# A decoder layer on one core: where the weight sums of four Strassen-type units are made, and which queue loads them

## The chip, the cores and the metric

The kernel runs on one core of one Trainium2 chip. A core has a matrix engine (TensorE; PE in the profile, with its weight loads as PEld), three engines for elementwise work (VectorE = DVE, ScalarE = ACT, GpSimd = POOL), an engine that only issues transfers (SyncE = SP), and 16 DMA engines that all queues share. Every engine works its instructions in the order in which they were compiled, and an instruction that waits holds up all that stand behind it on its engine. The metric is device microseconds of one execution, the median of the runs.

## What is computed

One layer of a hybrid decoder on 512 tokens with 1024 channels, all in fp32:

```python
h = layer_norm(x, ln_in_g, ln_in_b)
q_g, k_g, v_g, r_g, a_lr, q_lat, kv_lat, gate_logits = jnp.split(h @ w_in, offsets, axis=-1)
...
y_gla = (rms_norm(gla_chunked(q_g, k_g, v_g, log_a)) * jax.nn.silu(r_g)) @ w_o_gla
y_mla = merge_heads(o_mla) @ w_o_mla
g_gla, g_mla = jnp.split(jax.nn.sigmoid(gate_logits + b_gate), N_BRANCH, axis=-1)
mix = (g_gla * y_gla + g_mla * y_mla) @ w_out
h = layer_norm(DEEPNORM_ALPHA * h + mix, ln1_g[l], ln1_b[l])
ff = jnp.square(jax.nn.relu(h @ w_ff1[l])) @ w_ff2[l]
h = layer_norm(DEEPNORM_ALPHA * h + ff, ln2_g[l], ln2_b[l])
```

Four column blocks of `h @ w_in`, each 1024 wide, matter here: `r_g` (the kernel's unit "r"), `v_g` ("v") and the two halves of `gate_logits` ("a" and "b").

## The kernel before

**Precision.** Each fp32 product is made of three products of rounded parts: every operand is split into a high part (rounded by ScalarE) and a low part (the rest, by VectorE). `pump` (L167) does this for weights: it issues the load into a raw tile `wraw` (L178, three buffers), then `whi` on ScalarE (L190) and `wlo` on VectorE (L191). A stream entry that has a `src` takes an existing tile instead of a load. Units r and v split up to two entries ahead and put some of the parts into tiles `xh`, `xl`; units a and b split one entry ahead into the two `whi` and two `wlo` buffers.

**The four units.** `unit(sec, nxt)` (L711) multiplies one block by a scheme that needs seven products in place of eight (Strassen's, in Winograd's form). The weight block is cut into four quarters, "11", "12", "21", "22", each 512 rows by 512 columns, and each quarter into two halves (`hf`) of 512 KB. The seven products n = 0 to 6 use the weight operands of

```python
RPH = ("T1", "11", "22", "T2", "21", "T3", "T4")
```

T1 is made of quarters 12 and 11, T2 of T1 and 22, T3 of 22 and 12, T4 of T2 and 21. "11" and "21" come through `pump` as `wraw`; the others live in tiles `rw`. A sum is made in place, by a transfer that GpSimd's queue issues and that adds what it reads to the tile (`accum_op=ALU.add`, L623); T1 and "22" begin with a plain load that SP issues (L625). So T1's tile becomes T2 and then T4, and the tile of "22" becomes T3. Each sum has to wait until the split of the tile's former content is done.

The token operands S1 to S4 are made once, by `r_sums` (L649), on VectorE and ScalarE, and `keep` stores copies of them in DRAM. Unit r reads the tiles that `r_sums` made; the other units get copies back by `fetch` (L644), two transfers of 512 KB each, into new tiles.

The units run in the order r, v, a, b. Within a unit the steps are written after the products: after n = 0 the sum T2 (with 22) and `fetch("S2")`; after n = 2 the sum T3; at n = 3 the next unit's T1 loads and sums (`r_begin`) and, after it, the sum T4; at n = 6 the next unit's "22" loads.

**What runs beside them.** Between the products of the units, `tick` advances generators: the levels of the four GLA heads (`gla_levels`, L872) and their outputs (`gla_out`, L970). At one level of each head the next head's decay sums are made: `totals` (L853) is a chain of ever shorter adds on GpSimd (`tot`, L859) with an exponential on ScalarE at its end (L863), and `products` (L865) puts two adds and multiplies on GpSimd (`pr` L867, `qkp` L870) with a ScalarE copy between them. The levels themselves are an ScalarE copy `M` (L902), a product on PE (`px`, L937), and VectorE steps (L884, L909).

**Order.** A planner in the framework orders each engine's instructions when the kernel is built, by a timeline of its own in which the instruction written earlier goes first among those that are ready, and gives tiles their places from pools. Most tiles of these stages (rw, S, xh, xl and others) share one pool of 24 places of 4 KB in each partition; an allocation waits until a place is free, which is when all uses of the former tile are done.

Of the kernel before, what the change touches and what calls it, by code (L numbers as in the profile page):

```python
# [16 lines left out]
ALU = mybir.AluOpType  # L17
# [3 lines left out]
T = 512  # L21
# [31 lines left out]
def tile_hybrid_block(ctx: ExitStack, tc: tile.TileContext, I, out, dbg=None):  # L53
    nc = tc.nc
# [18 lines left out]
    def A(shape, dt=F32, n="a"):  # L73
        tag, bufs = ("C", 8) if n in TAG_C else (n, TAG_W[n]) if n in TAG_W else ("A", 24)
        return pa.tile(shape, dt, tag=tag, bufs=bufs, name=nm(n))
# [17 lines left out]
    def f(ap):  # L93
        return ap.bitcast(F32)

    act = nc.scalar.activation
    vtt = nc.vector.tensor_tensor
# [46 lines left out]
    stream = []  # L144
# [22 lines left out]
    def pump(i):  # L167
        while st["dma"] < min(len(stream), i + 1 + DMA_AHEAD):
            e = stream[st["dma"]]
            st["dma"] += 1  # L170
            if "src" in e:
                continue
            raw = A([P, e["nk"], T * 2 // e["nk"]], F32, "wraw")
            for sl, src, cw in e["dmas"]:
                dst = raw[:, sl, :e["n"]]
                if cw is not None:
                    dst = dst.rearrange("p (h c) -> p h c", c=cw)
                nc.sync.dma_start(dst, src)  # L178
            e["raw"] = raw
        while st["spl"] < min(len(stream), i + 2 + SPLIT_AHEAD):  # L180
            e = stream[st["spl"]]
            if st["spl"] > i + e.get("ahead", SPLIT_AHEAD) and not e["res"]:
                break
            nk, n = e["nk"], e["n"]
            hi, lo = [A([P, nk, T * 2 // nk], F32R, w) for w in HOME["a" if e["res"] else e.get("home", "w")]]
            raw = e["src"]() if "src" in e else e.pop("raw")
            with ExitStack() as gates:
                for g in st["gates"]:
                    gates.enter_context(tc.issue_after(g.ins))
                st["ins"] = act(hi[:, :nk, :n], raw[:, :nk, :n], AF.Copy)  # L190
                vtt(lo[:, :nk, :n], raw[:, :nk, :n], f(hi[:, :nk, :n]), op=ALU.subtract)  # L191
            st["gates"] = ()
            e["w"] = (hi, lo)
            st["spl"] += 1

    def weights(pl, k):
        per = pl["per"]
        i = pl["idx"][k // per]
        pump(i)
        hi, lo = stream[i]["w"]  # L200
        return hi[:, k % per, :], lo[:, k % per, :]
# [16 lines left out]
    def tick(width):  # L218
        for g in list(active[:width or WID[0]]):
            step(g)  # L220
# [35 lines left out]
    def gemm_tm(pls, xs, n, evac, width=None, tts=range(NT), guard=None, ks=None, accs=None, new=None, fine=False):  # L256
# [29 lines left out]
        for i, (tt, j) in enumerate(todo):  # L286
            evac(tt, j, accs[tt, j])
            if i == len(todo) // 2 - 1:
                pump(pls[-1]["idx"][-1] + 1)
# [3 lines left out]
    PL = {}  # L293
# [10 lines left out]
    RW = {}  # L304
# [6 lines left out]
    for sec, i in ORDER:  # L311
        if sec in UNITS:
            c0 = UCOL[sec]
# [302 lines left out]
    def r_load(sec, op, i, j, hf, add=False):  # L616
        w = I["w_in"].rearrange("(k p) n -> p k n", p=P)
        if not add:
            RW[sec, op, hf] = A([P, 2, T], F32, "rw")
        k0 = 4 * i + 2 * hf  # L620
        c0 = UCOL[sec] + j * T
        if add:
            nc.gpsimd.dma_start(RW[sec, op, hf], w[:, k0:k0 + 2, c0:c0 + T], accum_op=ALU.add)  # L623
        else:
            nc.sync.dma_start(RW[sec, op, hf], w[:, k0:k0 + 2, c0:c0 + T])  # L625

    def r_begin(sec):
        for hf in range(2):
            r_load(sec, "T1", 0, 1, hf)
        r_add(sec, "T1", "T1", 0, 0)  # L630

    def r_add(sec, dst, src, i, j):
        for hf in range(2):
            RW[sec, dst, hf] = RW[sec, src, hf]
            r_load(sec, dst, i, j, hf, add=True)
# [8 lines left out]
    def fetch(name):  # L644
        RS[name] = [A([P, 4, 256], F32R, name) for _ in range(2)]
        for d, w in zip(KEPT[name], RS[name]):
            nc.sync.dma_start(f(w), f(d))
# [63 lines left out]
    def unit(sec, nxt=None):  # L711
        a, b = [[MM() for _ in range(2)] for _ in range(2)]
        R = {}
        val, gate, later = sec == "v", sec in "ab", sec != "r"
# [15 lines left out]
        def put(key, t, o, scale=1.0):  # L730
            act(home(key, t), view(o), AF.Copy, scale=scale)

        def last(key, t, o, op):
            r = home(key, t)
            vtt(r, r, view(o), op=op)
            if val:
                if t == 0:
                    R["v" + key] = [A([P, 2, T], F32R, n) for n in ("vh", "vl")]
                split(r, *[w[:, t] for w in R["v" + key]])
# [24 lines left out]
        def lhs(n, k, t):  # L764
            c = slice(0, 256) if t is None else slice(t * P, (t + 1) * P)
            d = slice(256 + c.start, 256 + c.stop)
            if n in (1, 4):
                h = hT[k + 4 * (n == 4)]
                return h[:, 0, c], h[:, 1, c]
            if n == 6:  # L770
                return hT[k + 4][:, 0, d], hT[k + 4][:, 1, d]
            key = {0: "S1", 2: "S4", 3: "S2", 5: "S3"}[n]
            while not later and key not in RS:
                step(t_rs)
            return [w[:, k, c] for w in RS[key]]

        for n in range(7):
            o = a if n in (1, 3, 5) else b
            for hf in range(2):
                pump(PL[sec, n, hf])  # L780
                opens = n in (0, 1, 4, 6) and hf == 0
                for pp in range(2):
                    opens = opens and pp == 0
                    closes = hf == 1 and pp == 1
                    hi, lo = [w[:, pp] for w in stream[PL[sec, n, hf]]["w"]]
                    if gate:
                        xh, xl = lhs(n, 2 * hf + pp, None)
                        for q in range(4):
                            c = slice(q * P, (q + 1) * P)
                            d = o[q // 2][:, q % 2 * 256:][:, :256]  # L790
                            mm(d, hi[:, c], xh, start=opens and q % 2 == 0, stop=False, skip_group_check=True)  # L791
                            mm(d, hi[:, c], xl, start=False, stop=False, skip_group_check=True)  # L792
                            mm(d, lo[:, c], xh, start=False, stop=closes, skip_group_check=True)  # L793
                        continue
                    for t in range(2):
                        xh, xl = lhs(n, 2 * hf + pp, t)
                        mm(o[t], xh, hi, start=opens, stop=False, skip_group_check=True)
                        mm(o[t], xh, lo, start=False, stop=False, skip_group_check=True)
                        mm(o[t], xl, hi, start=False, stop=closes, skip_group_check=True)
                if hf == 0 and (later or n in (0, 2, 4, 6)):  # L800
                    tick(None)
                if n == 0 and hf == 1:
                    r_add(sec, "T2", "T1", 1, 1)
                    if later:
                        fetch("S2")
                if n == 2 and hf == 1:
                    r_add(sec, "T3", "22", 0, 1)
                    if later:
                        fetch("S3")
                if n == 3 and hf == 1:  # L810
                    r_add(sec, "T4", "T2", 1, 0)
                if n == 3 and hf == 0 and nxt:
                    r_begin(nxt)
                if n == 5 and hf == 1 and nxt:
                    fetch("S1")
                if n == 0 and hf == 0 and later:
                    fetch("S4")
                if n == 6 and hf == 0 and nxt:
                    for h2 in range(2):
                        r_load(nxt, "22", 1, 1, h2)  # L820
            for t in range(2):
                if n == 0:
                    put("22", t, o[t], -1.0)
                elif n == 1:
                    put("11", t, o[t])
                elif n == 2:
                    put("12", t, o[t], -1.0)
                elif n == 3:
                    last("12", t, o[t], ALU.subtract)
                elif n == 4:  # L830
                    last("11", t, o[t], ALU.add)
                elif n == 5:
                    put("21", t, o[t])
                    last("22", t, o[t], ALU.subtract)
                else:
                    last("21", t, o[t], ALU.add)
            if n < 6:
                tick(None)
# [762 lines left out]
```

## Time and profile before

| what | value |
|---|---|
| median of 3 runs | 871.78 us (870.83 to 871.88) |
| the profiled execution | 871.12 us, its span 869.3 us |
| mean granted clock of TensorE | 0.995 |
| VectorE, ScalarE, GpSimd busy | 72%, 56%, 22% of the span |
| HBM read and written | 116.64 MB and 12.58 MB |

The profile is one execution recorded by the hardware. A row of the timeline gives the start and the length in us, the engine, the line, what is written and read (`rw<-in_w_in_dram`), and in brackets how long the engine sat idle before it and which event ended that wait. "x3" merges three instructions in a row; "SPq" is an instruction of SP's queue, where the length is the issue, not the transfer. A row of the windows gives a stretch of time, then its length, then each engine's busy time in it with the number of instructions, the granted clock of TensorE as a share of the full one, the mean busy share of the 16 DMA engines, and GB/s.

### The profile page before, as it was taken

How to read it: one execution, taken by the hardware profiler on the slowest of the kernel's cores; microseconds unless marked ns; L12 is line 12 of the kernel's file. 1: busy time of each engine (PE TensorE's matmuls, PEld its weight loads, DVE VectorE, ACT ScalarE, POOL GpSimd, SP SyncE). 2: the span in 40 equal slices, each digit the busy share in tenths (PEclk: the TensorE clock that was granted, in tenths of full speed). 3: DMA queues.
4: the chain of work that ended last, by engine and by line, in shares of the span. 5: the costliest groups of instructions: out<-in, count | busy, mean ns of one | idle time of the engine just before them, and what ended most of it. 6: DMA issues, size and time to landing. Idle time of an engine off the chain costs nothing. (4 is left out here: it accounts for less than half of the span.)

```text
span 869.3 us, 12408 instructions
## 1 busy us (share of the span) xinstructions
PE 850.9 (98%) x4594; PEld 736.0 (85%) x4594; DVE 630.1 (72%) x1023; ACT 485.7 (56%) x830; POOL 189.4 (22%) x220
## 2 busy tenths in 40 slices
PE   8999998999999999999999999999999999999995
PEld 5988777889999989888888888988888888888884
DVE  7967978988776657567766888986567546854687
ACT  5367757757674635455555324485366446745662
POOL 2304651625222210000000021005301520331023
PEclk9999999999999999999999999999999999999998
DMA  7746899998997614123136355008922990497075
GB/s 239 220 122 225 238 294 258 296 312 219 292 252 178 206 35 125 31 55 104 49 142 215 129 156 209 1 1 252 260 69 49 290 220 23 86 315 180 1 193 97
DMA packets 80924, 144.19 MB, mean 166 GB/s; under 512 B 9153, under 2 KB 35188, under 8 KB 80864
## 3 DMA queue, kind: packets, MB, share of 16 engines
q1 hardware_dynamic: 56480, 87.63, 29.8%
q0 software_dynamic: 22464, 52.11, 27.9%
q10 hardware_dynamic: 1920, 3.66, 1.3%
q8 instruction: 36, 0.59, 0.3%
q14 instruction: 24, 0.20, 0.1%
HBM read 116.64 MB, written 12.58 MB: 149 GB/s over the span
## 5 line engine op out<-in xcount | busy, mean ns | idle before, releaser
L191 DVE TENSOR_TENSOR wlo<-wraw,whi 128x1024 fp32r<-128x1024 f32 (+3 forms) x82 | 91.6, 1118 | 91.3 <-ACT whi L190 91.0
L190 ACT ACTIVATE whi<-wraw 128x1024 fp32r<-128x1024 f32 (+3 forms) x82 | 78.6, 959 | 62.7 <-PE mm L242 31.7
L242 PE MATMUL mm<-h,whi 128*128 128x512 f32 x288 | 112.1, 389 | 0.0
L241 PE MATMUL mm<-h,whi 128*128 128x512 f32 x288 | 112.1, 390 | 0.0
L243 PE MATMUL mm<-h,wlo 128*128 128x512 f32 x288 | 107.2, 389 | 0.0
L1463 POOL DMA_DIRECT2D res<-ev x54 | 47.7, 995 | 237.9 <-ACT ev L1461 194.3
L623 POOL DMA_DIRECT2D rw<-in_w_in_dram x32 | 39.7, 1240 | 110.4 <-DVE wlo L191 43.0
L243 PEld LDWEIGHTS mm<-h,wlo 128*128 128x128 f32 x288 | 54.0, 188 | 11.3
L241 PEld LDWEIGHTS mm<-h,whi 128*128 128x128 f32 x288 | 54.1, 188 | 11.1
L242 PEld LDWEIGHTS mm<-h,whi 128*128 128x128 f32 x288 | 54.1, 188 | 11.1
L191 DVE TENSOR_TENSOR wlo<-rw,whi 128x1024 fp32r<-128x1024 f32 x32 | 40.7, 1271 | 16.0 <-ACT whi L190 15.7
L1528 ACT ACTIVATE relu<-mm 128x512 f32<-128x512 f32 x32 | 18.8, 595 | 57.2 <-PE mm L243 57.2
L190 ACT ACTIVATE whi<-rw 128x1024 fp32r<-128x1024 f32 x32 | 33.8, 1057 | 18.7 <-PE mm L792 10.3
L382 POOL TENSOR_TENSOR mv<-mv,mhalf 128x1 f32<-128x1 f32 x4 | 4.1, 1035 | 169.3 <-DVE mv L381 169.3
L190 ACT ACTIVATE xh<-wraw 128x1024 fp32r<-128x1024 f32 (+1 forms) x24 | 23.3, 979 | 26.5 <-PE mm L276 15.2
L791 PE MATMUL mm<-S,whi 128*128 128x256 f32 x128 | 36.3, 288 | 0.0
L792 PE MATMUL mm<-S,whi 128*128 128x256 f32 x128 | 35.7, 283 | 0.0
L793 PE MATMUL mm<-S,wlo 128*128 128x256 f32 x128 | 34.5, 285 | 0.0
L191 DVE TENSOR_TENSOR wlo<-wq,whi 128x1024 fp32r<-128x1024 f32 x15 | 18.3, 1223 | 20.4 <-ACT whi L190 20.4
L191 DVE TENSOR_TENSOR xl<-wraw,xh 128x1024 fp32r<-128x1024 f32 (+1 forms) x24 | 26.2, 1110 | 5.9 <-ACT xh L190 5.9
L902 ACT ACTIVATE M<-qk 128x256 f32<-128x256 f32 x56 | 23.9, 456 | 8.4 <-DVE qk L884 7.5
L1461 ACT ACTIVATE ev<-mm 128x512 f32<-128x512 f32 x20 | 11.9, 601 | 27.8 <-DMA res<-ev 19.3
(473 smaller groups left out, 2730.4 us busy)
## 6 DMA issues: line engine op xcount, KB each, us to landing
rw<-in_w_in_dram POOLq DMA_DIRECT2D x32, 512.0 KB, 8.0
wraw<-in_w_ff_dram SPq DMA_DIRECT2D x32, 512.0 KB, 8.1
wq<-in_w_ff_dram POOLq DMA_DIRECT2D x32, 512.0 KB, 9.7
res<-ev POOLq DMA_DIRECT2D x54, 256.0 KB, 8.4
wraw<-in_w_in_dram SPq DMA_DIRECT2D x24, 512.0 KB, 5.0
S<-S SPq DMA_DIRECT2D x24, 512.0 KB, 6.7
rw<-in_w_in_dram SPq DMA_DIRECT2D x16, 512.0 KB, 8.7
S<-s SPq DMA_DIRECT2D x8, 512.0 KB, 5.1
```

What stands on the lines that cost most here:

```text
L190: st["ins"] = act(hi[:, :nk, :n], raw[:, :nk, :n], AF.Copy)
L191: vtt(lo[:, :nk, :n], raw[:, :nk, :n], f(hi[:, :nk, :n]), op=ALU.subtract)
L241: mm(o, hi[:, c], xh, start=first, stop=False)
L242: mm(o, hi[:, c], xl, start=False, stop=False)
L243: mm(o, lo[:, c], xh, start=False, stop=last)
L623: nc.gpsimd.dma_start(RW[sec, op, hf], w[:, k0:k0 + 2, c0:c0 + T], accum_op=ALU.add)
L791: mm(d, hi[:, c], xh, start=opens and q % 2 == 0, stop=False, skip_group_check=True)
L792: mm(d, hi[:, c], xl, start=False, stop=False, skip_group_check=True)
L793: mm(d, lo[:, c], xh, start=False, stop=closes, skip_group_check=True)
L902: act(packed(M, s, i), half_lr(qk, s, i), AF.Copy)
L1463: nc.gpsimd.dma_start(res[tt + t][:, j * T:(j + 1) * T], e, accum_op=ALU.add)
L1528: act(r, ps, AF.Relu)
```

## The change

```diff
@@ pump
             raw = e["src"]() if "src" in e else e.pop("raw")
+            e["was"] = raw
@@ r_load
         c0 = UCOL[sec] + j * T
+        by = nc.sync if sec in "ab" else nc.gpsimd
         if add:
             nc.gpsimd.dma_start(RW[sec, op, hf], w[:, k0:k0 + 2, c0:c0 + T], accum_op=ALU.add)
         else:
-            nc.sync.dma_start(RW[sec, op, hf], w[:, k0:k0 + 2, c0:c0 + T])
+            by.dma_start(RW[sec, op, hf], w[:, k0:k0 + 2, c0:c0 + T])
@@ unit
-                if n == 0 and hf == 1:
+                if n == 0 and hf == 1 and not gate:
                     r_add(sec, "T2", "T1", 1, 1)
+                if n == 1 and hf == 0 and gate:
+                    for h2 in range(2):
+                        t = RW[sec, "T2", h2] = RW[sec, "T1", h2]
+                        vtt(t, t, RW[sec, "22", h2], op=ALU.add)
                     if later:
                         fetch("S2")
...
-                if n == 3 and hf == 1:
+                if n == 3 and hf == 1 and not gate:
                     r_add(sec, "T4", "T2", 1, 0)
+                if n == 4 and gate:
+                    t = RW[sec, "T4", hf] = RW[sec, "T2", hf]
+                    vtt(t, t, stream[PL[sec, 4, hf]]["was"], op=ALU.add)
```

In the gate units a and b, T2 and T4 are now made by VectorE from tiles that lie in SBUF anyway: T2 = T1 + 22 from the two `rw` tiles, T4 = T2 + 21 from the `rw` tile and the raw tile `wraw` of quarter 21, which `pump` now remembers as `was`. That takes eight accumulating transfers of 512 KB away from GpSimd's queue (two sums, two halves, two units) and puts eight adds of 128x1024 elements on VectorE. T1 and T3 are still made by transfers.

In units r and v, the plain loads of T1 and "22" (two halves each, two units: eight transfers) are issued by GpSimd in place of SP. Units a and b keep theirs on SP.

`fetch("S2")` stands below the new condition now. In a and b it comes one entry later than before. In unit v it is gone: v reads the S2 tiles that `r_sums` made for unit r, which therefore keep two places of the pool until v's product n = 3 is done, and two transfers of 512 KB are not made.

## The prediction, made before the changed kernel ran

> **What bounds the kernel now.** I read the page's first part, then the windows of the four units, then the waits of PE alone, and last the timelines of the engines around the only long wait. The chain of waits is of no use here: it covers 2 us at the end.
>
> ```profile
> span 869.3 us, 12408 instructions
> PE 850.9 (98%) x4594; PEld 736.0 (85%) x4594; DVE 630.1 (72%) x1023; ACT 485.7 (56%) x830; POOL 189.4 (22%) x220
> ```
>
> PE is busy in 98% of the span. Nothing but a shorter PE wait can make this kernel faster; nothing but a new one can make it slower. The change removes no matmul. So the question is where PE waits inside the units. The lines of the first products say when r, v and a begin (first and last start); b begins at 243.4 by the timeline:
>
> ```profile
> L797 PE MATMUL mm<-whi,s x16: 387/389/467, 94.7 to 129.1; 128*128 128x512 f32 x16
> L797 PE MATMUL mm<-whi,S x16: 389/389/476, 145.0 to 177.3; 128*128 128x512 f32 x16
> L791 PE MATMUL mm<-S,whi x128: 274/283/365, 188.0 to 284.2; 128*128 128x256 f32 x128
> ```
>
> The windows cut there, of r, v, a and b in this order, tell how much waiting there is:
>
> ```profile
> 94.70:145.00 50.30, 47.14 (x228) 39.37 (x229) 41.34 (x67) 32.72 (x57) 22.75 (x30) 0.97 0.93 261
> 145.00:188.00 43.00, 43.00 (x213) 36.20 (x211) 40.74 (x56) 29.94 (x54) 16.93 (x19) 1.00 1.07 296
> 188.00:243.40 55.40, 55.13 (x461) 54.61 (x460) 44.95 (x66) 38.97 (x78) 20.04 (x20) 1.00 0.96 263
> 243.40:292.00 48.60, 48.60 (x411) 48.60 (x410) 33.16 (x49) 31.46 (x59) 11.58 (x13) 1.00 0.81 196
> ```
>
> The first figure behind the comma is PE's busy time. Unit r lacks 50.30 - 47.14 = 3.16 us and ran at clock 0.97; a lacks 0.27; v and b lack nothing. The waits of PE between 80 and 300 us say on whom (total, times, longest):
>
> ```profile
> PE px L937 <- ACT M L902: 3.2, 1, 3.2
> PE mm L797 <- ACT s L111: 0.6, 1, 0.6
> PE mm L793 <- DVE wlo L191: 0.3, 1, 0.3
> ```
>
> One wait is nearly everything. The windows around it show that it also cost clock:
>
> ```profile
> 120.00:130.00 10.00, 9.53 (x44) 7.59 (x43) 5.38 (x7) 2.69 (x5) 4.21 (x6) 1.00 1.08 337
> 130.00:140.00 10.00, 7.31 (x29) 6.13 (x30) 6.94 (x11) 5.81 (x11) 0.34 (x2) 0.83 0.94 241
> ```
>
> At clock 0.83, ten microseconds do the work of 8.3: 1.7 us more. So the wait costs 3.16 + 1.7 = 4.9 us, 0.56% of the time. The windows of v, a and b stand at 1.00 in spite of the shorter waits of 0.3 us, so I take the halving to belong to a wait of about this length, and a wait of 0.8 us to cost no clock. The Trainium skill (TensorE: Matmul & The Clock Gate, "What's actually happening") puts the point at an idle window of about 3.4 us that runs freely; here 3.16 us were enough, so the row says that less will do.
>
> **Where the long wait comes from.** These are the timelines of POOL, SP, ACT and PE around it:
>
> ```profile
> 113.35 1.73 POOL L867 TENSOR_TENSOR pr<-qk 128x512 f32<-128x512 f32 x1
> 115.04 0.85 POOL L859 TENSOR_TENSOR tot<-tot 128x128 f32<-128x128 f32 x1
> 117.69 1.20 POOL L623 DMA_DIRECT2D rw<-in_w_in_dram  x1 [1.79 <-DVE xl L191]
> 118.47 1.17 POOL L859 TENSOR_TENSOR tot<-tot 128x64 f32<-128x64 f32 x1
> 124.93 1.20 POOL L623 DMA_DIRECT2D rw<-in_w_in_dram  x1 [5.29 <-DMA rw<-in_w_in_dram]
> 125.71 0.69 POOL L859 TENSOR_TENSOR tot<-tot 128x32 f32<-128x32 f32 x1
> 125.91 1.72 POOL L870 TENSOR_TENSOR qkp<-pr,qkp 128x512 fp32r<-128x512 f32 x1
> 128.42 1.20 POOL L623 DMA_DIRECT2D rw<-in_w_in_dram  x1 [0.78 <-DMA rw<-in_w_in_dram]
> 129.19 1.23 POOL L859 TENSOR_TENSOR tot<-tot 128x16 f32<-128x16 f32 x3
> 143.23 1.19 POOL L623 DMA_DIRECT2D rw<-in_w_in_dram  x1 [12.80 <-PE mm L799]
> ```
> ```profile
> 113.81 1.58 SPq L625 DMA_DIRECT2D rw<-in_w_in_dram  x2
> 123.54 0.90 SPq L625 DMA_DIRECT2D rw<-in_w_in_dram  x2
> ```
> ```profile
> 130.46 0.63 ACT L863 ACTIVATE tot<-tot 128x508 f32<-128x508 f32 x1 [7.77 <-POOL tot L859]
> 131.94 0.70 ACT L902 ACTIVATE M<-qk 128x256 f32<-128x256 f32 x2
> ```
> ```profile
> 132.69 1.02 PE L937 MATMUL px<-M 128*128 128x128 f32 x4 [3.16 <-ACT M L902]
> ```
>
> Read it from the end. PE waits 3.16 us for M; M stands on ACT behind the exponential L863, which waited 7.77 us for the last `tot`; the `tot` chain of head 1 stands on POOL behind two accumulating transfers, v's T1 sums (124.93 and 128.42), which each wait for the landing of the plain T1 load that SP issued at 113.81. POOL sat idle 5.29 us for the first and 0.78 for the second. The load flew about 124.93 - 113.81 = 11.1 us, in a stretch where the DMA engines are full (1.08).
>
> **The change, part by part.**
>
> *T1 and "22" loads of r and v on POOL.* The rows of the tile rw give an issue on either engine (ns, least, median, most):
>
> ```profile
> L623 POOL DMA_DIRECT2D rw<-in_w_in_dram x32: 1181/1203/2206, 38.3 to 268.2; - x32
> L625 SPq DMA_DIRECT2D rw<-in_w_in_dram x16: 383/418/637, 33.3 to 231.1; - x16
> ```
>
> Eight issues move: POOL gets 8 x 1.20 = 9.6 us, SP loses 8 x 0.42. r's four are hidden: the T1 pair falls into the time that POOL waits for those same loads (8.79 us before 38.34), the "22" pair into 4.39 us of idle POOL:
>
> ```profile
> 38.34 1.29 POOL L623 DMA_DIRECT2D rw<-in_w_in_dram  x1 [8.79 <-issue]
> 67.07 6.28 POOL L570 TENSOR_TENSOR g<-g,az 128x512 f32<-128x512 f32 x4 [25.87 <-ACT az L567]
> 77.74 2.96 POOL L517 TENSOR_TENSOR rs<-ss,mhalf 128x4 f32<-128x4 f32 x1 [4.39 <-DVE ss L515]
> ```
>
> If that cover went, rs would be up to 2.4 us late, and the transposes behind it. v's four are the heart of the matter. Its T1 pair must go out where SP issued it, at 113.81, so ahead of `pr` or just behind it at 115.04, in front of the rest of the `tot` chain. On the planner's timeline this makes the chain 2 x 1.20 = 2.4 us longer, and 4.8 if the "22" pair of 123.54 falls into it too. So the planner puts M and its product px later among PE's matmuls, or finds POOL free for `tot` before the T1 sums are ready. On the chip the chain's end is set by the landing, not by POOL's work: POOL idles 5.29 us of this stretch, enough for both issues. So PE should meet px some 2.4 us later while the chain ends about where it did: of 3.16 us some 0.8 stays, or nothing if `tot` goes ahead. Bounds for this step: a gain of 4.9 (wait and clock gone), and a loss if the load lands later, priced below. I take a gain of 4.9 - 0.8 = 4.1 as its lower, 4.9 as its upper likely value, and 4.5 for the sum.
>
> *S2 is not fetched in v.* Two of these transfers go, which v's full DMA engines (1.07) welcome, and PE waits for none of them:
>
> ```profile
> S<-S SPq DMA_DIRECT2D x24, 512.0 KB, 6.7
> ```
>
> Two pool places stay taken instead, from r's n = 3 on, so the "22" loads of 123.54 may find no place; POOL has 12.80 us of idle time before 143.23 in which to wait for one. Cost 0; without that cover the whole wait would fall on the T2 sums behind.
>
> *Eight sums on VectorE in a and b.* The same add of three SBUF tiles stands elsewhere in this kernel (L1448):
>
> ```profile
> L1448 DVE TENSOR_TENSOR T<-T,wq x8: 1215/1218/1221, 588.5 to 837.3; 128x1024 f32<-128x1024 f32 x8
> ```
>
> 8 x 1.22 = 9.8 us, 4.9 in each unit. Unit b has 48.60 - 33.16 = 15.4 us of idle VectorE, unit a 10.5. They hide, except perhaps a's two T4 sums, which can only run once the last split of T2 is done (the row of 213.18 further below ends at 215.68), in the second half of these windows:
>
> ```profile
> 210.00:220.00 10.00, 10.00 (x87) 10.00 (x86) 8.57 (x10) 7.43 (x14) 8.02 (x10) 1.00 0.80 156
> 220.00:230.00 10.00, 10.00 (x86) 10.00 (x85) 8.98 (x14) 6.39 (x16) 0.77 (x1) 1.00 1.05 338
> ```
>
> There 1.43 + 1.02 us are idle for 2.44 us of adds. `wlo` is then late by up to one add. Bounds: 0 and 2.4 us of PE wait; I take half an add, 0.6. One of the rows shows a second price, beside POOL's own reading:
>
> ```profile
> 212.53 2.06 POOL L870 TENSOR_TENSOR qkp<-pr,qkp 128x512 fp32r<-128x512 f32 x1
> 213.18 2.50 DVE L191 TENSOR_TENSOR wlo<-rw,whi 128x1024 fp32r<-128x1024 f32 x1 [0.41 <-ACT whi L190]
> ```
>
> A subtraction as large as the add above took 2.50 us beside POOL's qkp in place of some 1.2. The Trainium skill (SBUF — State Buffer, "SBUF: two separate sides") has the rule: a VectorE instruction with two SBUF inputs and a GpSimd instruction that reads SBUF lock each other out for a whole instruction. The row agrees; by that rule the four adds of unit a would cost up to 4 x 2.50 = 10 us of VectorE where they meet `tot`, and the 0.6 above would be nearer 2.4. Against it, the T2 and T4 sums of a leave POOL, the latter out of the midst of a `tot` chain. What they free is worth nothing by itself, since no PE wait of a hangs on it.
>
> **The sum**, against the profiled execution's own 871.12 us (1.8 us outside its span; it lies 0.66 below the median of 871.78): 871.12 - 4.5 + 0.6 = 867.2. Set against the median it is 867.9; I forecast **867.5**.
>
> **The rivals.**
>
> *The wait stays (no change).* The T1 sums stay in front of the chain, px stays at its place on PE, and the landing decides as before. For it: the sums are written ahead of `tot`, and the loads' flight hardly depends on who issues them. Against it: the planner's timeline gets 2.4 us longer at just this place. Time: 871.12 + 0.6 = 871.7, within a microsecond.
>
> *POOL's own issue makes it worse (slower).* POOL issues behind `pr`, at 115.04 in place of 113.81; with the same flight the T1 sums go out 1.2 us later, and if the "22" pair is then issued ahead of the last three `tot`, 2.4 more: the wait grows from 3.16 to 6.8 us, and a's crowded VectorE gives its 0.6. Time 871.12 + 3.6 + 0.6 = 875.3. It decides once the T1 loads land more than about a microsecond later than they did while px keeps its place on PE. For it: POOL works in order, and an issue there takes 1.20 us. Against it: fewer transfers share SP's ring.
>
> *VectorE becomes the bound in a.* All 2.4 us show and the long wait stays: 873.5. This belongs to the slower side too.
>
> **How the numbers follow.** The forecast case (wait shorter by 2 us or more, or gone) gets 0.45, the wait as it was 0.27, the two slower ones 0.28 (0.18 and 0.10). About 0.2% (1.7 us) is what a measurement of this kernel can tell from no change; so faster means under 870.0 and slower over 873.5. The likeliest case's own range is 865.5 to 869.5: 871.78 less 4.9, less the other 0.9 of PE's waits, is 866.0, and half a microsecond of scatter. The whole range reaches to the slower cases, 865.5 to 875.5.
>
> **What would show it.** Right: no PE wait over 1 us on M L902 in unit r and clock 1.00 in all windows of the unit; eight DVE adds of 1.22 us in a and b and PE still full there. Wrong: the same wait at another length with `tot` still behind a T1 sum; a PE wait for `wlo` of over 1 us between 205 and 240; or a POOL load that waits for a place in front of `tot`. A planner's order that differs in other stages could hide all this: then PE's idle time outside the units would have changed.

## The result, and the profile after

| | before | changed |
|---|---|---|
| median of the runs beside each other | 871.32 us (19 runs, 868.15 to 874.03) | 868.64 us (19 runs, 867.42 to 871.49) |
| ratio, with its 95% interval | | 0.9973 (0.9964 to 0.9982) |
| the profiled execution | 871.12 us | 868.45 us |
| HBM read | 116.64 MB | 111.40 MB |

The changed kernel is faster: by 2.7 us between the medians, by 0.27% (2.4 us) by the ratio. The forecast was 867.5 us, range 865.5 to 875.5. In the changed kernel the numbers of the lines have moved: M is L911 (before L902), its product px L946 (L937), the chain of totals L868 (L859) with its exponential L872 (L863), a sum made by a transfer L625 (L623), a plain load L627 (L625). The new adds are L809 (T2) and L820 (T4).

First the span and the busy time, from the first part of the page of the changed kernel:

```profile
span 866.7 us, 12380 instructions
PE 850.4 (98%) x4594; PEld 736.1 (85%) x4594; DVE 640.8 (74%) x1031; ACT 486.1 (56%) x830; POOL 189.4 (22%) x220
```

VectorE has 10.7 us more work, PE the same work in a span that is 2.6 us shorter. The waits of PE between 80 and 300 us (total, times, longest) say what went:

```profile
PE mm L793 <- ACT whi L191: 0.7, 1, 0.7
PE mm L799 <- ACT s L111: 0.6, 1, 0.6
PE mm L795 <- DVE wlo L192: 0.4, 1, 0.4
```

The wait of 3.2 us for M is gone, and two of 0.7 and 0.4 us for weight parts have come, both in unit a or at its end, where before there was one of 0.3 us. The windows around the place of the old wait, and two in unit a, of the changed kernel:

```profile
120.00:130.00 10.00, 10.00 (x47) 8.33 (x46) 10.00 (x13) 5.50 (x10) 7.05 (x10) 1.00 1.07 322
130.00:140.00 10.00, 10.00 (x52) 8.42 (x51) 7.47 (x12) 7.36 (x14) 1.54 (x3) 1.00 1.07 320
210.00:220.00 10.00, 9.65 (x80) 9.40 (x79) 10.00 (x13) 6.15 (x12) 2.31 (x2) 1.00 0.39 111
230.00:240.00 10.00, 9.26 (x77) 8.98 (x76) 8.37 (x16) 8.17 (x14) 1.82 (x2) 1.00 1.08 315
```

PE is full from 120 to 140 us and its clock is 1.00, where it was 9.53 and 7.31 at 1.00 and 0.83. In a, 0.35 and 0.74 us are missing instead.

To see where the rest went, I use the starts of four kinds of product as landmarks. These are the rows of the changed kernel (first and last start behind the durations), and the one of before that the prediction did not show:

```profile
L799 PE MATMUL mm<-whi,s x20: 387/389/476, 95.3 to 160.3; 128*128 128x512 f32 x20
L799 PE MATMUL mm<-whi,S x12: 389/389/476, 140.6 to 173.3; 128*128 128x512 f32 x12
L793 PE MATMUL mm<-S,whi x128: 278/283/387, 183.9 to 281.6; 128*128 128x256 f32 x128
L242 PE MATMUL mm<-ogT,whi x64: 387/389/496, 294.6 to 370.0; 128*128 128x512 f32 x64
```
```profile
L241 PE MATMUL mm<-ogT,whi x64: 387/389/496, 297.2 to 372.6; 128*128 128x512 f32 x64
```

| stretch | before | changed | difference |
|---|---|---|---|
| start to r's first product | 94.7 | 95.3 | +0.6 |
| r (to v's first product) | 50.3 | 45.3 | -5.0 |
| v (to a's first product) | 43.0 | 43.3 | +0.3 |
| a and b (to the first ogT product) | 109.2 | 110.7 | +1.5 |
| from there to the end of the span | 572.1 | 572.1 | 0 |
| sum | 869.3 | 866.7 | -2.6 |

Unit r gained 5.0 us, as much as the wait with its half clock was priced at. Three stretches gave 2.4 us back. The +0.6 of the start can't be told from scatter: over the kernels below this start lies between 94.5 and 95.4 us, at 94.7 in one with the same loads on GpSimd (experiment 1) and at 95.4 in one that moves no load at all (experiment 4). It goes with the clock. These are the windows from 16 to 20 us, before and changed:

```profile
16.00:20.00 4.00, 4.00 (x26) 4.00 (x25) 4.00 (x9) 3.10 (x6) 2.61 (x4) 1.00 0.70 251
```
```profile
16.00:20.00 4.00, 4.00 (x24) 4.00 (x24) 3.89 (x9) 3.59 (x7) 2.72 (x4) 0.93 0.78 282
```

Over 10 to 20 us the profiled execution of the changed kernel has clock 0.83, that of before 1.00. The same lowered clock stands there in experiments 4, 5, 8 and 9 (starts of 94.8 to 95.4 us) and in none of the others (94.5 to 95.0).

**How the wait went.** These are GpSimd and ScalarE of the changed kernel around it, and the product on PE:

```profile
115.68 0.77 POOL L627 DMA_DIRECT2D rw<-in_w_in_dram  x1
117.54 0.74 POOL L627 DMA_DIRECT2D rw<-in_w_in_dram  x1 [1.09 <-DMA latd<-latT]
...
124.11 1.21 POOL L625 DMA_DIRECT2D rw<-in_w_in_dram  x1 [1.18 <-DMA rw<-in_w_in_dram]
125.89 1.20 POOL L625 DMA_DIRECT2D rw<-in_w_in_dram  x1 [0.57 <-DMA rw<-in_w_in_dram]
126.64 2.95 POOL L868 TENSOR_TENSOR tot<-tot 128x32 f32<-128x32 f32 x4
```
```profile
126.62 0.72 ACT L911 ACTIVATE M<-qk 128x256 f32<-128x256 f32 x2 [1.01 <-DVE qk L893]
129.63 0.63 ACT L872 ACTIVATE tot<-tot 128x508 f32<-128x508 f32 x1 [2.29 <-POOL tot L868]
```
```profile
130.02 0.60 PE L946 MATMUL px<-M 128*128 128x128 f32 x4
```

The end of the chain of totals still stands behind v's two T1 sums, and these still wait for the landing. The exponential still waits for the chain: it starts at 129.63, 0.83 us ahead of the 130.46 of before. And px still has its place: it runs 130.02 - 95.3 = 34.7 us behind r's first product, and before PE was ready for it at 132.69 - 3.16 = 129.53, 34.8 us behind. What is new is one order on ScalarE. M stood behind the exponential before; now it stands in front of it, at 126.62, and is ready 2.7 us before PE wants it.

So the theory after the result, which the experiments bear out only in part: **the whole gain is this order, and the eight sums take about 1.5 us of it back.** The rivals: the gain comes from an earlier landing of the loads on GpSimd's queue, or from the lighter traffic; the sums are free, and what was given back is the next wait behind the removed one.

### The profile page after: what moved, and what is told of

The parts are those of the page before. It is cut to its first block, busy times and chain, and to the rows that moved or that the text cites. A ratio compares the mean times of both kernels' runs of the same rounds, so it can differ in the third digit from the quotient of the medians.

```text
span 866.7 us, 12380 instructions
## 1 busy us (share of the span) xinstructions
PE 850.4 (98%) x4594; PEld 736.1 (85%) x4594; DVE 640.8 (74%) x1031; ACT 486.1 (56%) x830; POOL 189.4 (22%) x220
## 3 DMA queue, kind: packets, MB, share of 16 engines
HBM read 111.40 MB, written 12.58 MB: 143 GB/s over the span
## 5 line engine op out<-in xcount | busy, mean ns | idle before, releaser
L192 DVE TENSOR_TENSOR wlo<-wraw,whi 128x1024 fp32r<-128x1024 f32 (+3 forms) x82 | 90.3, 1102 | 86.3 <-ACT whi L191 86.2
L625 POOL DMA_DIRECT2D rw<-in_w_in_dram x24 | 29.1, 1217 | 95.9 <-DVE wlo L192 26.8
L911 ACT ACTIVATE M<-qk 128x256 f32<-128x256 f32 x56 | 24.0, 457 | 9.0 <-DVE qk L893 8.2
```

Source lines behind the costliest of these rows:

```text
L911: act(packed(M, s, i), half_lr(qk, s, i), AF.Copy)
```

## The experiments

All were timed in runs beside the kernel before. Beside the ratio stand, in us, the lengths of r and v together, of a and b together, and of all four units, in one profiled execution each, from the same landmarks as above:

| kernel | ratio (95%) | r and v | a and b | all four |
|---|---|---|---|---|
| before | 1 | 93.3 | 109.2 | 202.5 |
| changed | 0.9973 (0.9964 to 0.9982) | 88.6 | 110.7 | 199.3 |
| 1: loads on GpSimd only | 0.9981 (0.9971 to 0.9990) | 89.2 | 110.2 | 199.4 |
| 2: eight sums only | 1.0026 (1.0013 to 1.0039) | 92.4 | 111.0 | 203.4 |
| 3: S2 of r read by v only | 1.0007 (0.9996 to 1.0017) | 90.7 | 109.1 | 199.8 |
| 4: exponentials behind M only | 0.9975 (0.9965 to 0.9985) | 90.3 | 109.2 | 199.5 |
| 5: totals one level earlier only | 0.9971 (0.9961 to 0.9982) | 90.3 | 109.6 | 199.9 |
| 6: changed, exponential ahead of M | 0.9990 (0.9981 to 0.9999) | 90.3 | 110.5 | 200.8 |
| 7: changed, no sums on VectorE | 0.9972 (0.9960 to 0.9984) | 90.0 | 109.3 | 199.3 |
| 8: changed, only b's sums | 0.9967 (0.9950 to 0.9984) | 88.8 | 109.7 | 198.5 |
| 9: changed, a's T4 by transfer | 0.9970 (0.9958 to 0.9982) | 88.8 | 110.1 | 198.9 |
| 10: changed, a's sums made three times | 1.0010 (0.9999 to 1.0022) | 88.9 | 114.7 | 203.6 |
| 1, 3 and 5 together | 0.9972 (0.9961 to 0.9983) | 88.8 | 110.0 | 198.8 |

**Experiment 1: the loads of r and v on GpSimd's queue, nothing else.**

```diff
+        by = nc.sync if sec in "ab" else nc.gpsimd
-            nc.sync.dma_start(RW[sec, op, hf], w[:, k0:k0 + 2, c0:c0 + T])
+            by.dma_start(RW[sec, op, hf], w[:, k0:k0 + 2, c0:c0 + T])
```

> Edit: only the queue part of the change (plain loads of T1 and 22 of units r and v issued by GpSimd); the eight sums stay transfers, S2 is fetched in v. Theory (the long wait of unit r ends because the moved loads bring head 1's exponential behind the last level copy M on ScalarE): the 3.16 us wait and the 1.7 us of clock go, nothing is given back in unit a: 4.5 to 5.5 us under the kernel before, about 866.3, 2 us faster than the whole change. Rival (the wait went because v fetches no S2, or because the sums left GpSimd): this kernel stays within 1 us of before, with the wait on M still there.

868.58 us. The wait of r is gone here too, and M stands ahead of the exponential on ScalarE (at 125.94 and 128.94 us). The queue part alone brings the new order; the sums and S2 aren't needed for it. The time missed what I expected: 2.5 us below the kernel before in place of 4.5 to 5.5, and no better than the whole change. I had expected nothing to be given back without the sums, but v is 0.9 us longer than before and a and b take 110.2 us without any sum on VectorE, 1.0 more than before.

**Experiment 2: the eight sums of a and b on VectorE, nothing else** (S2 is fetched as before, all loads on SP).

```diff
-                    r_add(sec, "T2", "T1", 1, 1)
+                    if not gate:
+                        r_add(sec, "T2", "T1", 1, 1)
...
+                        vtt(t, t, RW[sec, "22", h2], op=ALU.add)
...
+                    vtt(t, t, stream[PL[sec, 4, hf]]["was"], op=ALU.add)
```

> Edit: only the eight sums on VectorE in units a and b; all plain loads on SP, S2 fetched as before. Theory: the long wait of r stays (3.2 us, clock below 1.00), and unit a pays for its crowded VectorE: 1 to 2.5 us slower than before, about 873. Rival (the sums are free, and the change gained less than 4.9 us for another reason, such as the start of the program): within 0.7 us of before.

873.26 us, 2.3 us slower by the ratio, as expected. These are the waits of its PE between 80 and 300 us:

```profile
PE px L946 <- ACT M L911: 2.3, 1, 2.3
PE mm L792 <- ACT whi L191: 0.7, 1, 0.7
...
PE mm L794 <- DVE wlo L192: 0.4, 1, 0.4
```

The old wait is there, and behind it the same two waits of 0.7 and 0.4 us that the changed kernel has. The traffic that the sums save (112.45 MB read in place of 116.64) buys nothing that shows; what they add to a and b does, 1.8 us in this profile.

**Experiment 3: v reads r's S2 tiles, nothing else.**

```diff
                     r_add(sec, "T2", "T1", 1, 1)
-                    if later:
+                    if gate:
                         fetch("S2")
```

> Edit: unit v reads the S2 tiles that r_sums made and fetches none; all else as before. Theory: nothing waits for these transfers and the places held are not missed: within 0.7 us of before, the wait of r still there. Rival (the two transfers fewer, or the places they leave, make the difference in r or v): 2 us or more either way.

870.89 us: no change that can be measured. Its profiled execution took only 868.94 us with the wait still there, and shows one way in which single executions with this wait differ. Its product px, its window behind the wait, and the same window of experiment 2, whose wait on M was 2.3 us:

```profile
131.68 0.71 PE L937 MATMUL px<-M 128*128 128x128 f32 x4 [2.14 <-ACT M L902]
```
```profile
130.00:140.00 10.00, 8.32 (x41) 7.03 (x42) 8.95 (x15) 7.88 (x15) 0.00 (x0) 1.00 1.07 320
```
```profile
130.00:140.00 10.00, 8.27 (x33) 6.82 (x34) 8.01 (x13) 6.28 (x13) 0.00 (x0) 0.83 1.03 284
```

A wait of 2.14 us cost no clock in one execution, and one of 2.3 us cost 1.7 us (10 x 0.17) in another. The length of the wait hangs on a landing, and whether the clock is halved isn't settled by the length alone.

With the wait still there but the clock full, the four units of this execution take 199.8 us, about as long as in the changed kernel (199.3) and in experiment 4 (199.5), which don't have it. So most of the difference to the 202.5 us of before is the half clock and the longer wait of that one execution. The timed executions point the same way. Those of the kernel before with a mean granted clock of 0.997 (11 beside the experiments) took 868.0 to 869.8 us, median 869.0; those at 0.992 or less (23) took 871.1 to 876.1, median 871.9. The changed kernel at 0.997 or more (7) took 867.4 to 869.6, median 868.3. At this clock the two differ by 0.7 us, not 2.7. The mean is taken over the whole execution, so it doesn't say where the clock was lost.

**Experiment 4: the kernel before, with one order changed.** The two exponentials of the next head are issued after the copy that makes M of level 64, in every head; loads, sums and S2 are as before.

```diff
-        act(GL[h], GL[h], AF.Exp, scale=1.0 / 16.0)
-        act(t[:, :o], t[:, :o], AF.Exp, scale=1.0 / 16.0)
+        def exps():
+            act(GL[h], GL[h], AF.Exp, scale=1.0 / 16.0)
+            act(t[:, :o], t[:, :o], AF.Exp, scale=1.0 / 16.0)
+        return exps
...
-                totals(h + 1)
+                late = totals(h + 1)
...
+            if s == 64 and h + 1 < GH:
+                with tc.issue_after(st["pack"].ins):
+                    late()
```

> Edit: kernel before, with the two exponentials of a head's decay sums put behind the last level copy M of the head before (order on ScalarE alone; no queue, sum or fetch changed). Theory (ScalarE's order is the whole cause of the wait): the wait of 3.16 us and the half clock go as in q_only, 4 to 5 us under before, with the T1 loads landing as late as before. Rival (the earlier landing of the loads on GpSimd's queue is needed): the wait on M goes but PE meets another one of 1 us or more behind it, less than 3 us gained.

868.66 us, as the changed kernel, but 2.4 us below the kernel before where I had expected 4 to 5. ScalarE of this kernel:

```profile
124.36 0.73 ACT L904 ACTIVATE M<-qk 128x256 f32<-128x256 f32 x2 [1.47 <-DVE qk L886]
...
130.69 0.63 ACT L864 ACTIVATE tot<-tot 128x508 f32<-128x508 f32 x1 [5.09 <-POOL tot L859]
```

Here the chain ends even later than before (the exponential starts at 130.69 in place of 130.46), with all loads on SP and all sums by transfers. No faster landing and no lighter queue is in it; an order of a few instructions on one engine, written by hand, gives the same time as the change. (The planner also put px a little earlier here, 128.28 - 95.4 = 32.9 us behind r's first product; M is ready at 125.1.) The two kernels are equal in the end because each gives back something else. This one makes r and v 3.0 us shorter (93.3 to 90.3) and leaves a and b alone; the changed one makes them 4.7 shorter and loses 1.5 in a and b. The waits of PE in this one:

```profile
PE mm L797 <- ACT s L111: 1.1, 2, 0.6
PE mm L798 <- DVE wlo L191: 1.0, 1, 1.0
```

The second stands at v's second product. PE comes there 3.6 us earlier than before (v's first product starts at 141.4 in place of 145.0) and meets a low part of v's weights that isn't ready. That is the next wait behind the removed one, and it is what I had written for the rival: a wait of 1 us or more behind the removed one, and less than 3 us gained. It comes for the larger part from a landing. ScalarE's split of v's T1 waits for the transfer that makes the sum; first the changed kernel, then this one:

```profile
137.26 1.06 ACT L191 ACTIVATE xh<-rw 128x1024 fp32r<-128x1024 f32 x1 [0.93 <-DMA rw<-in_w_in_dram]
```
```profile
138.40 1.06 ACT L190 ACTIVATE xh<-rw 128x1024 fp32r<-128x1024 f32 x1 [0.17 <-DMA rw<-in_w_in_dram]
```

With r's first product at 95.3 and 95.4 us the split starts 1.1 us later here, and the low part 1.75 us later (141.85 in place of 140.10). So the order alone is enough for the measured time, but not for all that r and v gained in the changed kernel: there the T1 sum landed sooner and took the next wait away as well. The loads on GpSimd's queue don't bring that in every execution: in experiments 6 and 7, which have them, PE waits 0.8 us at this place.

**Experiment 5: the kernel before, with the totals handed out one level earlier.**

```diff
-            if s == 16 and h + 1 < GH:
+            if s == 8 and h + 1 < GH:
                 totals(h + 1)
                 products(h + 1, QK[h + 1])
```

> The kernel before, with head 1's totals and products handed out one level earlier (s = 8 in place of 16), so that GpSimd makes the whole chain of totals ahead of v's two first sums (T1); the exponential still stands in front of M on ScalarE, and loads, sums and S2 are as before. Theory (M waits for the exponential only because the chain of totals stands behind the landing of the T1 loads): no wait over 0.5 us on M, 867.5 to 869 us, as the change. Rival (the exponential in front of M costs by itself, or the work handed out earlier crowds r's VectorE and ScalarE): a wait of 1 us or more in r, 870 to 872 us.

868.03 us, as expected. GpSimd and ScalarE of this kernel:

```profile
115.22 3.34 POOL L859 TENSOR_TENSOR tot<-tot 128x128 f32<-128x128 f32 x5
...
120.54 1.11 POOL L859 TENSOR_TENSOR tot<-tot 128x4 f32<-128x4 f32 x1
124.35 1.20 POOL L623 DMA_DIRECT2D rw<-in_w_in_dram  x1 [2.70 <-PE px L937]
126.35 1.20 POOL L623 DMA_DIRECT2D rw<-in_w_in_dram  x1 [0.80 <-DMA rw<-in_w_in_dram]
```
```profile
122.13 0.63 ACT L863 ACTIVATE tot<-tot 128x508 f32<-128x508 f32 x1
122.64 0.73 ACT L902 ACTIVATE M<-qk 128x256 f32<-128x256 f32 x2
...
125.70 0.73 ACT L902 ACTIVATE M<-qk 128x256 f32<-128x256 f32 x2 [1.05 <-DVE qk L884]
```

The whole chain is done ahead of the T1 sums at 124.35 and 126.35, so the exponential waits for nothing, although it stands in front of both M. This is the other leg of the cause: the exponential hurt only because its chain stood behind the two landings. Again a wait for a low part, of 0.8 us, comes at v's second product, and r and v take 90.3 us as in experiment 4.

**Experiment 6: the changed kernel, with M of level 64 of head 0 issued behind the exponential again.**

```diff
-        act(t[:, :o], t[:, :o], AF.Exp, scale=1.0 / 16.0)
+        st["exp"] = act(t[:, :o], t[:, :o], AF.Exp, scale=1.0 / 16.0)
...
+                with ExitStack() as behind:
+                    if s == 64 and h == 0:
+                        behind.enter_context(tc.issue_after(st["exp"].ins))
+                    act(packed(M, s, i), half_lr(qk, s, i), AF.Copy)
```

> The change, with one order on ScalarE put back: the copy that makes head 0's last M (level 64) is issued behind the exponential of head 1's totals, as before the change. Loads of r and v stay on GpSimd's queue, sums stay on VectorE. Theory (this order is the whole cause; the exponential of the changed kernel started at 129.63 us, px stood at 130.02 and came 2.23 us behind the exponential's start before): a wait of px on M of about 1.8 us in unit r, 869.5 to 870.5 us, over 1 us above the change. Rival (the loads on GpSimd's queue brought the gain by landing earlier): no wait over 0.5 us on M, as the change, 868.3 to 868.9 us.

869.56 us: by the ratios 1.5 us slower than the changed kernel (the two intervals just touch). The time is the one that I had expected, but that is luck, for it did not come about in the way that I had expected. The wait that I expected on M, 1.8 us, measured 0.2, which is the rival's sign:

```profile
PE mm L800 <- DVE wlo L192: 0.8, 1, 0.8
PE mm L793 <- ACT whi L191: 0.7, 1, 0.7
...
PE px L949 <- ACT M L914: 0.2, 1, 0.2
```
```profile
128.91 0.63 ACT L872 ACTIVATE tot<-tot 128x508 f32<-128x508 f32 x1 [3.73 <-POOL tot L868]
129.44 0.71 ACT L914 ACTIVATE M<-qk 128x256 f32<-128x256 f32 x2
```
```profile
131.18 0.60 PE L949 MATMUL px<-M 128*128 128x128 f32 x4
```

The order of ScalarE is the old one, and M comes late as I had worked out: px could run 2.27 us behind the exponential's start. But the planner knew of it and put px later: 131.18 - 94.9 = 36.3 us behind r's first product in place of 34.7. With px at its old place the wait would have been the 1.6 us between. So with the loads on GpSimd and this order held, the planner has another cure, and most of the old wait stays away; r and v are still 1.7 us longer than in the changed kernel, half of it the 0.8 us at v's second product. By the ratios 0.17% of the 0.27% went with the order and 0.10% stayed: the order carries the larger part of the changed kernel's gain, not all of it.

**Experiment 7: the changed kernel with no sum of a or b on VectorE** (experiments 1 and 3 together).

> The change without its eight VectorE sums: loads of r and v on GpSimd's queue, v reads r's S2 tile, the second and fourth sums of a and b stay accumulating transfers. Theory (the order on ScalarE gives the whole gain, the sums cost 1.5 to 2 us of it): wait on M of unit r gone, 866.5 to 867.5 us, that is 1 to 2 us below the change's 868.6. Rival (the sums cost nothing in the change; the remaining 868.6 is what the order alone gives): 868.3 to 868.9 us.

867.78 us, between what I had written for the theory and for the rival. The ratio is the changed kernel's (0.9972 and 0.9973), so the time alone doesn't tell the two apart; the medians differ by 0.9 us, but they come from different rounds, each with its own runs of the kernel before. In the landmarks a and b take 109.3 us, as before the change, but r and v take 1.4 us more than in the changed kernel, and all four units the same 199.3.

With all eight sums on VectorE a and b take 110.5 to 111.0 us (changed, 2 and 6). Without any they take 109.1 to 109.6 in five kernels, and 110.0 and 110.2 in the two (1, and 1, 3 and 5 together) in which PE comes to a's first product as early as in the changed kernel, at 183.9 us. So beside kernels that reach a at the same time the sums cost 0.5 to 0.7 us, and the rest of the 1.5 can be the price of coming early. Only alone (experiment 2) do they show in the time.

**Experiments 8 and 9: fewer sums on VectorE.** In the first the four sums of a stay transfers, in the second only a's two T4 sums do.

The edit of the second is this; the first does the same for T2 as well.

```diff
-                if n == 3 and hf == 1 and not gate:
+                if n == 3 and hf == 1 and sec != "b":
                     r_add(sec, "T4", "T2", 1, 0)
-                if n == 4 and gate:
+                if n == 4 and sec == "b":
```

> The change, but the four sums of unit a stay accumulating transfers; only b's are on VectorE. Theory (the cost of the sums sits in a, where VectorE has no idle time between 201 and 221 us): waits of a at 210 and 235 us gone, about 867.2 us, 1.5 us below the change. Rival (cost sits in b or there is none): as the change, 868.3 to 868.9 us.

> The change, but a's two fourth sums (T4) stay accumulating transfers; its second sums are on VectorE. Theory (the crowded place is that of T4, 207 to 213 us): about as without any sum of a on VectorE, 867.2 us. Rival (T2's sums or GpSimd's chain in a cost it): as the change, 868.6 us.

868.38 and 867.69 us. I had expected 867.2 of both; the first median stands where its rival put it, the second between its two, and all of it lies within the intervals, so the times decide nothing. By the landmarks a and b together take 109.7 us with b's sums alone, 110.1 with a's T2 as well, and 110.7 with a's T4 too. Each step has a part, of some 0.4 to 0.6 us; my theory that T4 alone is the crowded one isn't borne out. One profile each is thin for differences of 0.4 us (109.7 with b's sums is less than the 110.0 and 110.2 without any), so this split stays open.

**Experiment 10: the changed kernel, with each of a's four sums made as add, subtract, add.** (The edit for T2; that for T4 is alike.)

```diff
-                        vtt(t, t, RW[sec, "22", h2], op=ALU.add)
+                        for op in (ALU.add, ALU.subtract, ALU.add) if sec == "a" else (ALU.add,):
+                            vtt(t, t, RW[sec, "22", h2], op=op)
```

> The change, with each of the four VectorE sums of unit a made as add, subtract, add: eight more instructions of 1.2 us or more, 9.8 us of VectorE in a. Theory (VectorE is full in a, so what is added there shows on TensorE): 4 us or more above the change, 872.5 us or more, with waits on wlo in the first product of the high rows. Rival (a hides its sums): within 1 us of the change, 868 to 869.6 us.

871.86 us, 3.2 us above the changed kernel, a little under the 4 us that I had expected and far above the rival's 1 us. Most of what PE waits for between 180 and 300 us are these four:

```profile
PE mm L795 <- DVE wlo L192: 2.2, 4, 1.0
```

The eight further instructions are 9.8 us of adds (VectorE's busy time rose by 6.5, from 640.8 to 647.3 us, as others took less), and 4.0 us show in a and b (114.7 against 110.7). So a has little room for adds: by the landmarks its first 4.9 us cost about 1.0 (110.7 against 109.7 in experiment 8), the next 9.8 cost 4.0.

**A faster version.** A kernel with experiments 1, 3 and 5 together (loads on GpSimd, S2 from r, totals one level earlier) was run as a candidate:

> The loads of r and v on GpSimd's queue, r's S2 tile read by v, no sums on VectorE, and head 1's totals handed out one level earlier (s = 8). A candidate for the fastest: if the 0.8 us wait for wlo at v's second product (141 us without the earlier totals) goes with it, 867 us; if the two cures do not add, as without it, 867.5 to 868.2 us.

868.34 us, ratio 0.9972 (0.9961 to 0.9983). It is no better than either alone: the cures of one wait don't add. Here M stands behind the exponential again (128.58 and 128.04 us), and PE doesn't wait for it, because the chain ends sooner. None of the kernels with ratios from 0.9967 to 0.9981 can be told from the changed one by its time, though experiment 5 reaches the same with one number of the source changed.

**What this leaves of the theory.** That the exponential ahead of M, behind a late chain, makes the long wait is shown from two sides (4 and 5). That the changed kernel's whole gain is the order is too much: without it, 0.10% of 0.27% stays (6), and with it alone another microsecond is lost in v, for the larger part to a landing (4). That the sums take 1.5 us back isn't shown: beside kernels that come to a equally early the profiles give 0.5 to 0.7 us, and the times of 1 and 7 show nothing of it. And a good part of what any cure buys is the clock that the wait costs in most executions (3).

## Why the prediction was right, step by step

- **What bounds the kernel: right for the execution that was read.** One wait in r with its half clock was priced at 4.9 us, and r became 5.0 us shorter when it went. But 4.9 us is the price in an execution that loses the clock, and r, v, a and b together became only 3.2 us shorter. With the clock kept and a wait of 2.1 us still there, the four units took 199.8 us against 199.3 in the changed kernel (experiment 3).
- **Where the wait comes from: right, and now shown.** M behind the exponential (experiment 4 takes M out and the wait on it goes), the exponential behind the chain, the chain behind the T1 sums (experiment 5 takes the chain out and the wait on M falls to 0.2 us).
- **How the change would remove it: wrong.** The step that failed is the one in which the planner "puts M and its product px later among PE's matmuls, or finds POOL free for `tot` before the T1 sums are ready". Neither happened. I held M's place behind the exponential as given and looked for movement on PE and GpSimd. The planner moved it on ScalarE. Experiment 6 shows that the first of my two ways is what it does once that is barred. Why its timeline turned the two around wasn't tried; that the two issues lengthen the chain on it, so that M is ready first, is only argued. The price of the step, 4.5 us, was near the 5.0 of r because both ways end in a wait that is gone: in that the forecast was lucky. The conditions of the rival in which the wait stays all held (the T1 sums in front of the chain, px at its place, the landing deciding when the chain ends), and yet the wait went, by an order that neither case had looked at.
- **Landing and issue: partly wrong in size.** I priced a plain load on GpSimd at 1.20 us by the row of the sums. The rows of the changed kernel tell the two apart, and together with the eight loads' mean of 0.76 us the eight issues take 6 us in place of 9.6:

```profile
L625 POOL DMA_DIRECT2D rw<-in_w_in_dram x24: 1194/1208/1313, 37.0 to 257.1; - x24
L627 POOL DMA_DIRECT2D rw<-in_w_in_dram x8: 733/760/782, 29.8 to 130.7; - x8
```

  The flight wasn't "the same" either: from the issue at 115.68 to the first sum at 124.11 it is 8.4 us, against 11.1 before, and for the second load 8.4 (117.54 to 125.89) against some 14 (113.81, one of two issues merged there, to 128.42). This shorter flight made up for the later issue, and so the rival in which GpSimd's issue makes it worse, which needed a load that lands later, fell with the changed kernel itself and again in experiment 1 (T1 sums at 123.02 and 125.28 us).
- **S2 at no cost: right** (experiment 3).
- **The sums: mis-sized alone, not settled beside the other parts.** I took 0.6 us, all of it in a, between bounds of 0 and 2.4. In the changed kernel a and b together are 1.5 us longer than before, of which 0.5 to 0.7 is left beside kernels that reach a as early; by experiment 8, 1.0 belongs to a's sums, so not all of it to T4. Alone the sums cost 1.8 us by the profile and 2.3 by the times (0.26%, 0.13 to 0.39). The sign that I had named, PE still full in a, didn't come: 0.35 and 0.74 us are missing there. The rows of the adds:

```profile
L809 DVE TENSOR_TENSOR rw<-rw,rw x4: 1216/1222/1262, 184.8 to 244.6; 128x1024 f32<-128x1024 f32 x4
L820 DVE TENSOR_TENSOR rw<-rw,wraw x4: 1208/1260/2143, 207.7 to 266.7; 128x1024 f32<-128x1024 f32 x4
```

  Most cost about the 1.22 us of the quoted add. The long one and a split beside it are these, on VectorE and GpSimd of the changed kernel:

```profile
203.75 3.07 DVE L192 TENSOR_TENSOR wlo<-rw,whi 128x1024 fp32r<-128x1024 f32 x1
...
211.32 2.14 DVE L820 TENSOR_TENSOR rw<-rw,wraw 128x1024 f32<-128x1024 f32 x1
```
```profile
203.98 1.75 POOL L876 TENSOR_TENSOR pr<-qk 128x512 f32<-128x512 f32 x1
205.24 5.89 POOL L868 TENSOR_TENSOR tot<-tot 128x128 f32<-128x128 f32 x6
211.08 1.30 POOL L879 TENSOR_TENSOR qkp<-pr,qkp 128x512 fp32r<-128x512 f32 x1
```

  The Trainium skill (SBUF — State Buffer, "SBUF: two separate sides") has a VectorE instruction with two SBUF inputs and a GpSimd instruction that reads SBUF lock each other out for a whole instruction. These rows agree for two VectorE instructions, of 3.07 and 2.14 us; the other sum of this stretch took 1.31 us beside the same chain. The 2.4 us of wait that the prediction drew from that rule is above the 1.0 that a's sums cost by the landmarks, and my 0.6 is below it.
- **What is late next: left out.** The prediction named no wait behind the removed one. There is one, at v's second product: 1.0 us in experiment 4, 0.8 in 5, 6 and 7. The changed kernel has none there that the list of waits shows, but its v is 0.3 us longer, and without any sums a and b take longer in the kernels in which PE comes to them early (experiment 7).
- **The sum.** Against the profile I forecast -4.5 + 0.6 = -3.9 us and got -2.7. The gain in r was 0.5 better; a and b took 0.9 more than the sums were given, v 0.3, and the scatter of the start 0.6.

## What to carry to other kernels

Where several engines each work in order, a wait that ends in one late landing can be taken away at any link of its chain, and often by order alone: look for an instruction that doesn't need the late thing but stands behind one that does (here M behind an exponential), and move that, before moving transfers. When a change to a planned kernel is judged, compare the compiled order on every engine around the wait, not only on those that the change names. And price what the removed wait was hiding: PE arrives at the next stage that much earlier, and the first thing there that was just in time is late. Last, read a wait's price from several executions: here a good part of it was a halved clock, which came with some executions and not with others.

## What the runs showed of the hardware

- On GpSimd's queue a plain load of 512 KB took 0.76 us to issue and one that adds to its target 1.21 us (the two rows of the tile rw above).
- The clock was halved beside a wait of 2.3 us in one execution and not beside one of 2.14 us in another. The Trainium skill (TensorE: Matmul & The Clock Gate, "What's actually happening") tells of an idle window of about 3.4 us that runs freely; that both occur agrees with a window that runs freely, but waits clearly shorter than it were enough here. In both halved executions the clock was down for about 3.4 us, from about 133 us, 0.3 us behind the end of the wait in the kernel before (132.69) and 1.4 behind it in experiment 2 (131.73).
- The kernel with the long wait scatters more than those without: 868.15 to 874.03 us over 19 runs against 867.42 to 871.49 for the changed one, and 868.41 to 869.85 over 11 runs for experiment 4. That goes with the clock: the kernel before took 869.0 us (median) at a mean granted clock of 0.997 and 871.9 at 0.992 or less.
